# The head of the first mixer: chunks in another order, first K group in halves, sums kept in PSUM, one pass through SBUF

## The chip, the cores and the metric

The kernel is one program on one core of a Trainium2 chip. The metric is the device time of one execution in microseconds (us). A core has five engines with an instruction stream each: TensorE (PE) for matmuls, VectorE (DVE) and ScalarE (ACT) for elementwise work, GpSimdE (POOL), and SyncE (SP), which here only issues DMA transfers. Each engine runs its stream in program order and waits on semaphores that other engines and transfers raise.

## The reference

A trunk of two layers works on one sequence of 256 frames with 2048 features, all in float32. Each layer is a mixer and an MLP, each behind a modulated norm. Cut to what the change touches:

```python
c_act = jax.nn.silu(c)
mod = jnp.einsum('bd,de->be', c_act, mod_w[layer]) + mod_b[layer]
sh1, sc1, g1, sh2, sc2, g2 = jnp.split(mod, 6, axis=-1)
h = rms_norm(x, norm_mix_w[layer]) * (1.0 + sc1) + sh1
...
proj = jnp.einsum('btd,de->bte', h, w_in)
gq, gk, gv, gz, gb, ga, aq, ak, av = split_sizes(proj, AB_SPLITS)
o_a = gated_deltanet(gq, gk, gv, gz, gb, ga, ...)
o_b = chunk_band_attention(aq, ak, av, ...)
x = x + g1 * (concatenate([o_a, o_b]) @ w_out)
```

The head of the first mixer is everything up to the end of `proj`: norm, the first modulation sums, and the product of h with a 2048 x 7184 matrix, in column blocks of 512. The rest (output projection, MLP, the second layer with a state-space mixer) is the same in both kernels.

## The kernel before, in words

**Products.** x lies in SBUF with features on partitions, as four tiles `x[cb]` of 512 features. The contraction over 2048 features is cut in four K groups (`kg` 0 to 3). A weight block of 512 columns comes as four chunks, one for each K group; a chunk is 128 x 2048 float32, 1 MB. There are 14 blocks: the gated-delta ones (GK, GQ, GV, GZ and each +1, told below as k0, q0, v0, k1, q1, v1) as "b" chunks, whose products lie with features on partitions, and the attention ones (AQ, AK, AV and +1: aq, ak, av, aq1 and so on) as "a" chunks, with frames on partitions. A product is done at full precision in one of two ways. *Split*: the weight half (128 x 1024) is cast by ACT to a short type, `wh` (L317), DVE subtracts that from the raw half to get the rest, `wl` (L321), and the same is done to the activations (a unit `u` with high and low part); then PE runs three matmuls for one product, 256 columns wide for b, 512 for a. *Whole*: one float32 matmul on the raw chunk and the unsplit activation `hw`; the trace records each float32 matmul of a b chunk twice. `loader` loads and splits a chunk, `b_item` and `a_item` emit it.

**Modulation.** A column f of modulation vector v is a sum over a 128 x 2048 row of 1 MB with silu(c), broadcast as `crow`: `mod_job` loads the row and DVE does it in one instruction with an accumulator (L439). The head needs shift (v = 0) and scale (v = 1) for 16 columns each, four columns for each K group. In the beginning eight rows are summed, then `norm_unit` makes group 0's unit in the steps L862 (x times scale times R, the inverse norm), L864 (ACT adds the shift) and L865 (the low part).

**Order.** Then for K group 0, 1 and 2 come eight chunks, in the order k0, q0, v0, k1, q1, v1, aq, ak. k0 and q0 keep their sums in PSUM (`held`); for the other six the product of each group is taken out to SBUF, copied by ACT the first time (L1590) and added by DVE the two other times (L1592). Between the chunks the generator `modgen` loads and sums a modulation row for each chunk, eight for the next K group. The last group (from `partial_item(3, 0)`) ends each block in turn: a convolution for b blocks, a norm and transposes for a blocks, and then the delta-rule and attention work as background tasks between chunks. Other blocks (av, aq1, ak1, av1, GZ, GZ+1) run all four chunks there, one after the other.

**Buffers and queues.** Raw chunks and modulation rows share a pool of four buffers of 1 MB (`rawp`); all of them are loaded through SP's queue, in program order, and a load waits at SP's head until the last reader of its buffer is done. Only `pin` and `pin_mod` fix the order of a few instructions; else a scheduler with priorities (`self.priority(20)` for sums) places them on DVE and ACT.

Of the kernel before, what the change touches and what calls it, by code (L numbers as in the profile page):

```python
# [10 lines left out]
F32 = mybir.dt.float32  # L11
# [101 lines left out]
class Trunk:  # L113
# [8 lines left out]
    def __init__(self, tc, ctx, ins, out):  # L122
# [7 lines left out]
        self.u_p = pool("up", 18)  # L130
# [9 lines left out]
        self.ahead = []  # L140
        self.pin_mod = 0
# [174 lines left out]
    def split_steps(self, src, hi, lo, pin=False):  # L316
        a = self.nc.scalar.copy(hi, src)  # L317
        if pin:
            self.tc.keep_in_program_order(a)
        yield  # L320
        b = self.nc.vector.tensor_tensor(lo, src, hi.bitcast(F32), op=ALU.subtract)  # L321
        if pin:
            self.tc.keep_in_program_order(b)
        yield
# [13 lines left out]
    def constants(self):  # L338
# [7 lines left out]
        cact = self.const([P, 16], "cact")  # L346
# [21 lines left out]
    def constants2(self):  # L368
# [3 lines left out]
        for n, f in (("gconv", 0.5), ("gnw", 0.5), ("sconv", 0.5), ("sconv_b", 0.5), ("qnw", P ** -0.5)):  # L372
            nc.vector.tensor_scalar(col(n), col(n), f, None, op0=ALU.mult)
# [50 lines left out]

    def mod_job(self, layer, vs, fs, step):


        nc = self.nc
        key = ("mix", layer) if vs[0] < 3 else ("mlp", layer)
        for f0 in range(fs.start, fs.stop, step):  # L430
            s = slice(f0, f0 + step)
            for f in range(f0, f0 + step):
                for v in vs:
                    t = self.mod[v % 3, key]
                    raw = self.raw_p.tile([P, 2048], F32, tag="raw", name=self.nm("mraw"))
                    nc.sync.dma_start(raw, self.i["mod"][layer, v, f])
                    yield
                    with self.priority(20):
                        x = nc.vector.scalar_tensor_tensor(raw, raw, 1.0, self.crow, op0=ALU.mult, op1=ALU.mult, accum_out=t[:, f : f + 1])  # L439
                    if self.pin_mod > 0:  # L440
                        self.pin_mod -= 1
                        self.tc.keep_in_program_order(x)
                    if f < s.stop - 1 or v != vs[-1]:
                        yield
            for v in vs:
                t = self.mod[v % 3, key][:, s]
                nc.vector.tensor_tensor(t, t, self.modb[:, layer, v, s], op=ALU.add)
                if v % 3 == 1:
                    nc.vector.scalar_tensor_tensor(t, t, 1.0, self.nw[key][:, s], op0=ALU.add, op1=ALU.mult)
                self.ready[v % 3, key] = f0 + step  # L450
# [22 lines left out]
    def loader(self, src, whole=False):  # L473
# [4 lines left out]
        res = []  # L478

        def load():  # L480
            raw = self.raw_p.tile([P, 2048], F32, tag="raw", name=self.nm("raw"))
            nc.sync.dma_start(raw, src)
            for hf in range(2):
                r = raw[:, 1024 * hf : 1024 * hf + 1024]
# [16 lines left out]
    def b_item(self, ps, src, act, first, last, after=None, whole=False):  # L501

        load, ws = self.loader(src, whole)

        def run():
            o_, (u, x) = ps(), act()
            for hf, (wh, wl) in enumerate(self.tiles(ws, 512)):
# [301 lines left out]
    def sumsq(self, cb, b, late=False):  # L809
# [3 lines left out]
        x = self.x[cb][:, 2 * b : 2 * b + 2]  # L813
        if cb == 3:
# [34 lines left out]
    def norm_unit(self, r, cb, key, acts, whole=False):  # L849
# [4 lines left out]
        x = []  # L854
        for b in range(2):
            h = self.s2([P, 2, SEQ], tag="hf")
            if whole:
                x.append(self.s2([P, 2, SEQ], tag="hw"))
            for f in range(2):
# [6 lines left out]
                if whole:  # L866
                    nc.scalar.activation(x[b][:, f], h[:, f], AF.Identity, bias=shift[:, col])
            if b == 0:
                yield
        acts.append((p, x))  # L870
# [63 lines left out]
    def conv(self, ps, tiles, w, bias, part=None):  # L934

        nc = self.nc
        dst = self.unit()
# [294 lines left out]
    def att_qk(self, ps, nw, part=None):  # L1232
# [19 lines left out]
        res = self.unit()  # L1252
# [9 lines left out]
    def att_v(self, ps):  # L1262
        v = self.unit(shape=[P, 2, 4, P])
        for t in range(2):
            self.nc.scalar.copy(v[:, t].rearrange("p h d -> p (h d)"), ps[t])
# [271 lines left out]
    def run(self):  # L1537
# [7 lines left out]
        for layer in range(2):  # L1545
            self.mod_start(layer)
        for t in range(4):
            nc.sync.dma_start(self.x[t].rearrange("p f t -> p (f t)"), i["x"][t])
        for cb in range(4):
            for b in range(2):  # L1550
                self.sumsq(cb, b)
        first = self.mod_job(0, (0, 1), range(0, 4), 2)
# [259 lines left out]
```

## Time and profile before

| | us |
|---|---|
| runs of the kernel before, median (lowest, highest) | 2715.22 (2714.29, 2719.38) |
| the profiled execution | 2719.37 |
| its span, first to last instruction | 2717.6 |
| PE busy in the span | 2665.0 |
| mean granted TensorE clock | 0.998 |

The page of the profile gives the busy time of each engine, the chain of work that ended last, and groups of instructions. A timeline row reads: start, duration, engine, line, operation, out<-in, shapes, count, and in brackets the idle time ahead of it with what ended it. A row of the windows view reads: stretch and its length, then for PE, PEld (PE's weight loads), DVE, ACT and POOL the busy time with the number of instructions in brackets, the granted clock, the DMA share and GB/s. A row of the chain of waits reads: start, duration, what was on the chain.

### The profile page before, as it was taken

To read this page: it belongs to the slowest core of one execution; us is meant where nothing else is said; L and a number is where in the kernel's file an instruction comes from. 1 tells how busy PE (TensorE), PEld (TensorE's weight loads), DVE (VectorE), ACT (ScalarE), POOL (GpSimd) and SP (SyncE) were. 2 spreads that over 40 slices of the span, in tenths; PEclk is the share of its full clock that TensorE was granted. 3 is DMA by queue.
4 is the path that set the end of the run, shared out by engine and by line. 5 is a ranking of instruction groups with operands and counts; after the bars stand their busy time and mean duration, and the time that the engine had idled before them with its cause. 6 is when DMAs were issued, how large, how long until landed. Compare 5 with 4: busy or idle time off the path is not lost.

```text
span 2717.6 us, 39677 instructions
## 1 busy us (share of the span) xinstructions
PE 2665.0 (98%) x15664; PEld 2350.4 (86%) x15664; DVE 2147.6 (79%) x3081; ACT 1351.2 (50%) x1976; POOL 24.5 (1%) x98
## 2 busy tenths in 40 slices
PE   5999999999999999999999999999999999999999
PEld 5887989888888888888888888888888888888888
DVE  7998998987888888889889876897777855555554
ACT  3444454546445354454556544665555354454452
POOL 1000000000000000000000000000000000000000
PEclk9999999999999999999999999999999999999999
DMA  9986487867899898988456665554558855555554
GB/s 341 353 325 235 172 301 272 294 241 282 322 339 328 328 336 330 333 331 307 165 185 217 217 234 200 203 185 172 196 177 293 324 201 188 188 191 193 186 192 134
DMA packets 100459, 680.06 MB, mean 250 GB/s; under 512 B 11185, under 2 KB 14513, under 8 KB 19377
## 3 DMA queue, kind: packets, MB, share of 16 engines
q1 hardware_dynamic: 95376, 669.07, 68.5%
q10 hardware_dynamic: 4896, 8.46, 1.0%
q8 instruction: 123, 2.02, 0.3%
q14 instruction: 64, 0.52, 0.1%
HBM read 675.33 MB, written 2.16 MB: 249 GB/s over the span
## 4 chain that ended last, share of the span: by engine, by line
PE 90%; DVE 6%; DMA 1%; ACT 1%; issue 1%; SPq 0%; ACTq 0%; DVEq 0%
PE pw L308 70%; PE pg L308 13%; PE pm L311 4%; PE pm L308 3%; DVE mraw L439 2%; DVE wl L321 1%; PE pm L314 1%; DMA mraw<-in_mod_dram 1%; DVE u L1592 0%; ACT wh L317 0%; DVE hf L862 0%; ACT pm L1042 0%; DMA raw<-in_w_ab_dram 0%; DMA x<-in_x_dram 0%; DVE u L865 0%
## 5 line engine op out<-in xcount | busy, mean ns | idle before, releaser
L317 ACT CAST wh<-raw 128x1024 fp32r<-128x1024 f32 x870 | 907.1, 1051 | 1031.6 <-PE pw L308 732.9
L321 DVE TENSOR_TENSOR wl<-raw,wh 128x1024 fp32r<-128x1024 f32 x870 | 1048.7, 1220 | 463.8 <-ACT wh L317 349.6
L308 PE MATMUL pw<-u,wh 128*128 128x512 f32 x5584 | 1321.6, 391 | 2.6 <-DVE pad L973 1.9
L308 PEld LDWEIGHTS pw<-u,wh 128*128 128x128 f32 x5584 | 1032.2, 188 | 208.2 <-issue 3.3
L308 PEld LDWEIGHTS pw<-u,wl 128*128 128x128 f32 x5584 | 702.3, 191 | 21.3 <-issue 2.1
L308 PE MATMUL pw<-u,wl 128*128 128x256 f32 x5584 | 714.5, 283 | 0.3 <-DVE wl L321 0.3
L439 DVE SCALAR_TENSOR_TENSOR mraw<-mraw,crow 128x2048 f32<-128x2048 f32 x192 | 438.0, 2283 | 17.8 <-DMA mraw<-in_mod_dram 17.5
L308 PE MATMUL pg<-wh,u 128*128 128x512 f32 x864 | 281.6, 397 | 0.0
L308 PEld LDWEIGHTS pg<-wh,u 128*128 128x128 f32 x864 | 161.9, 188 | 32.1 <-issue 0.5
L925 DVE SCALAR_TENSOR_TENSOR x<-pw,mod,x 128x256 f32<-128x256 f32 x352 | 161.1, 478 | 22.6 <-PE pw L308 20.3
L308 PE MATMUL pg<-wl,u 128*128 128x512 f32 x432 | 169.9, 393 | 0.7 <-DVE wl L321 0.5
L308 PE MATMUL pg<-u,wh 128*128 128x256 f32 x672 | 124.6, 285 | 0.0
L308 PEld LDWEIGHTS pg<-u,wh 128*128 128x128 f32 x672 | 105.7, 192 | 0.3
L308 PEld LDWEIGHTS pg<-wl,u 128*128 128x128 f32 x432 | 81.4, 188 | 17.6 <-DVE wl L321 2.1
L308 PE MATMUL pg<-u,wl 128*128 128x256 f32 x336 | 95.3, 284 | 0.0
L308 PE MATMUL pm<-u,wh 128*128 128x256 f32 (+1 forms) x304 | 64.6, 310 | 19.2 <-ACT wh L317 19.2
L308 PEld LDWEIGHTS pm<-u,wh 128*128 128x128 f32 x304 | 49.1, 198 | 20.3 <-ACT wh L317 20.0
L308 PEld LDWEIGHTS pg<-u,wl 128*128 128x128 f32 x336 | 64.4, 192 | 0.1
L984 DVE SCALAR_TENSOR_TENSOR u<-pad,cst,u 128x256 f32<-128x256 f32 x144 | 60.6, 477 | 3.3 <-ACT u L978 3.2
L864 ACT ACTIVATE u<-hf,mod 128x256 fp32r<-128x256 f32 x64 | 29.3, 502 | 53.0 <-DVE hf L862 53.0
L1504 ACT ACTIVATE rl<-rs 128x512 f32<-128x512 f32 x64 | 40.4, 632 | 18.9 <-DVE rs L1499 14.4
L308 PE MATMUL pm<-u,wl 128*128 128x256 f32 x176 | 46.1, 290 | 3.1 <-DVE wl L321 3.1
(299 smaller groups left out, 1580.5 us busy)
## 6 DMA issues: line engine op xcount, KB each, us to landing
raw<-in_w_dram SPq DMA_DIRECT2D x256, 1024.0 KB, 5.0
mraw<-in_mod_dram SPq DMA_DIRECT2D x192, 1024.0 KB, 6.0
raw<-in_w_ab_dram SPq DMA_DIRECT2D x56, 1024.0 KB, 5.7
raw<-in_w_ssd_dram SPq DMA_DIRECT2D x48, 1024.0 KB, 4.9
raw<-in_w_sz_dram SPq DMA_DIRECT2D x32, 1024.0 KB, 4.9
raw<-in_wo_ssd_dram SPq DMA_DIRECT2D x32, 1024.0 KB, 4.8
raw<-in_wo_ab_dram SPq DMA_DIRECT2D x16, 1024.0 KB, 5.2
sE<-sd_rowd ACTq DMA_DIRECT2D x32, 256.0 KB, 4.9
```

The costliest lines, as they stand in the source:

```text
L308: self.nc.tensor.matmul(o, a, b, start=start, stop=stop, skip_group_check=True)
L311: self.nc.tensor.matmul(o, lhsT, rhs, start=True, stop=True, skip_group_check=True)
L314: self.nc.tensor.transpose(o, a, self.ident[:k, :k])
L317: a = self.nc.scalar.copy(hi, src)
L321: b = self.nc.vector.tensor_tensor(lo, src, hi.bitcast(F32), op=ALU.subtract)
L439: x = nc.vector.scalar_tensor_tensor(raw, raw, 1.0, self.crow, op0=ALU.mult, op1=ALU.mult, accum_out=t[:, f : f + 1])
L864: nc.scalar.activation(hi, h[:, f], AF.Identity, bias=shift[:, col])
L925: nc.vector.scalar_tensor_tensor(x[:, 2 * b + f], ps[:, f, n], g[:, 2 * cb + f : 2 * cb + f + 1], x[:, 2 * b + f], op0=ALU.mult, op1=ALU.add)
L984: nc.vector.scalar_tensor_tensor(h, pad[:, f, 1 + q : 257 + q], w[:, q, j : j + 1], h, op0=ALU.mult, op1=ALU.add)
L1504: nc.scalar.activation(rl, lo, AF.Relu)
```

## The change

The head is written anew. The parts:

- One more buffer in the pool of units (18 to 19). A flag `in_order` fixes the order on SP, DVE and ACT as written, until the first chunk of the last group. A flag `in_units` has weight chunks of K groups 0 and 1 loaded as two halves of 0.5 MB into buffers of the unit pool, not of `rawp`; from group 2 on they go to `rawp` again.
- Before the first product four modulation rows are loaded in place of eight (columns 0 and 1). Scale column 0 comes from an extra input `mod0`, the same weights turned, and is summed by PE in 16 matmuls with one column each (`mod_pe`); `mod_sum` is the DVE sum, `mod_fin` adds bias and factors.
- Group 0's unit is made by `norm_first`: x times R on DVE, scale and shift by ACT into `hw`, then the split. Its first half (256 features) suffices for the first halves of the chunks k0, q0, v0 and k1, which run first. Columns 2 and 3 are summed between them.
- Sequence, eight chunks a group: group 0 the second halves of v0 and k1, then of k0 and q0, then q1, v1, aq, ak; group 1 aq, ak, k0, q0, av (K group 0 and 1) and aq1 (0 and 1); group 2 av, aq1, k0, q0, v0 (1 and 2), k1 (1 and 2). So v0, k1, q1, v1, aq, ak, av and aq1 pass through SBUF once each, by an ACT copy; their last add is part of the block's end.
- The last group goes k0, q0, v0, n_item (the narrow block of gates), k1, aq (2 and 3), ak (2 and 3), av, q1 (1 to 3), v1 (1 to 3), aq1, and then as before.
- Whole chunks: five before, at the last group of k1, q1, v1, aq and ak. Ten after, two of them as two halves: the first halves of k0 and v0, q1 and aq in group 0, aq in group 1, av in group 2, and in the last group k0, k1, aq, q1 and v1.

```diff
-        self.u_p = pool("up", 18)
+        self.u_p = pool("up", 19)
...
+    def mod_pe(self, raw, o):
+        for k in range(16):
+            self.mmx(o, raw[:, k * P : k * P + P], self.cact[:, k : k + 1], k == 0, k == 15)
...
+            if units:
+                raw = [self.unit(shape=[P, 1024]) for _ in hfs]
+                for hf, r in zip(hfs, raw):
+                    self.dma(r, src[:, 1024 * hf : 1024 * hf + 1024])
+            else:
+                raw = self.raw_p.tile([P, 2048], F32, tag="raw", name=self.nm("raw"))
+                self.dma(raw, src)
+                raw = [raw[:, 1024 * hf : 1024 * hf + 1024] for hf in hfs]
...
+    def norm_first(self, cb, key, acts, now=False):
...
+        for b in range(2):
+            self.ordered(nc.vector.tensor_tensor(x[b], self.x[cb][:, 2 * b : 2 * b + 2], self.row(self.R, 2), op=ALU.mult))
+            if now and b == 0:
+                yield
+        yield
+        for b in range(2):
+            for f in range(2):
+                col = slice(cb * 4 + 2 * b + f, cb * 4 + 2 * b + f + 1)
+                self.ordered(nc.scalar.activation(x[b][:, f], x[b][:, f], AF.Identity, scale=scale[:, col], bias=shift[:, col]))
+            self.split(x[b], p[b][:, :, 0], p[b][:, :, 1])
...
+            for n, (name, k, keep) in enumerate(seq):
+                chunk(name, k, n in whole, (1,) if kg == 0 and n < 4 else (0, 1), keep)
+                if n == 0:
+                    self.tail()
+                due = n if kg else (0, 1, 1, 2, 4, 5, 7, 7)[n]
+                load(due + 2)
+                if n == 3:
+                    unit.step()
+                sums(due)
...
+        chunk("k0", 0, True, (0,))
+        raws = [self.mod_load(mod[0, 0, 2])]
+        chunk("q0", 0, False, (0,))
+        raws.append(self.mod_load(mod[0, 1, 2]))
+        self.mod_sum(raws[0], 0, 0, 2)
+        chunk("v0", 0, True, (0,))
+        raws += [self.mod_load(mod[0, v, 3]) for v in range(2)]
+        self.mod_sum(raws[1], 0, 1, 2)
...
+        chunk("k1", 0, False, (0,))
+        for v in range(2):
+            self.mod_sum(raws[2 + v], 0, v, 3)
...
+        group(0, [("v0", 0, False), ("k1", 0, False), ("k0", 0, True), ("q0", 0, True),
+                  ("q1", 0, False), ("v1", 0, False), ("aq", 0, True), ("ak", 0, True)], (4, 6))
+        group(1, [("aq", 1, False), ("ak", 1, False), ("k0", 1, True), ("q0", 1, True),
+                  ("av", 0, True), ("av", 1, True), ("aq1", 0, True), ("aq1", 1, True)], (0,))
+        self.in_units = False
+        group(2, [("av", 2, False), ("aq1", 2, False), ("k0", 2, True), ("q0", 2, True),
+                  ("v0", 1, True), ("v0", 2, True), ("k1", 1, True), ("k1", 2, True)], (0,))
...
+        chunk("k0", 3, True)
+        self.tail()
+        self.in_order = False
+        chunk("q0", 3)
+        chunk("v0", 3)
         self.n_item(i["w_gb"], get, 16, self.gdn_gates)
+        chunk("k1", 3, True)
+        for kg in (2, 3):
+            chunk("aq", kg, kg == 3)
+        for kg in (2, 3):
+            chunk("ak", kg)
```

In `group` the third entry of a chunk says that its sum stays in PSUM, and the last argument lists the whole chunks by place.

SP's loads in the first group of the changed kernel (mraw are modulation rows, u from in_w_ab the half chunks of q0, v0, k1 and then v0's second half):

```order
L454 DMA mraw_274<-in_mod_dram 128x2048
L454 DMA u_276<-in_w_ab_dram 128x1024
L454 DMA mraw_292<-in_mod_dram 128x2048
L454 DMA u_295<-in_w_ab_dram 128x1024
L454 DMA mraw_323<-in_mod_dram 128x2048
L454 DMA mraw_325<-in_mod_dram 128x2048
L454 DMA u_331<-in_w_ab_dram 128x1024
```

Weights and rows now alternate from the first chunk on, where before eight rows stood ahead of the first weight chunk; k1's half (u_331) is behind both rows of column 3.

DVE in the same place, from the split of k1's half on (wl are the low parts of weights, mod_123 and mod_124 the shift and the scale, u_217 the low part of the second half of group 0's unit):

```order
L323 TENSOR_TENSOR wl_334<-u_331,wh_333 128x1024
L435 SCALAR_TENSOR_TENSOR mraw_323,mod_123<-mraw_323,crow 128x2048
L435 SCALAR_TENSOR_TENSOR mraw_325,mod_124<-mraw_325,crow 128x2048
L448 TENSOR_TENSOR mod_123<-mod_123,cst 128x1
L448 TENSOR_TENSOR mod_124<-mod_124,cst 128x1
L450 SCALAR_TENSOR_TENSOR mod_124<-mod_124,cst 128x1
L323 TENSOR_TENSOR u_217<-hw_219,u_217 128x2x256
```

Both sums of column 3 now stand between the split of k1's first half and the unit's second half.

SP's loads in group 2, first before, then of the changed kernel (raw are weight chunks of 1 MB):

```order
L482 DMA raw_1276<-in_w_ab_dram 128x2048
L436 DMA mraw_1312<-in_mod_dram 128x2048
L482 DMA raw_1339<-in_w_ab_dram 128x2048
L436 DMA mraw_1373<-in_mod_dram 128x2048
L482 DMA raw_1400<-in_w_ab_dram 128x2048
```

```order
L454 DMA raw_1041<-in_w_ab_dram 128x2048
L454 DMA mraw_1075<-in_mod_dram 128x2048
L454 DMA mraw_1077<-in_mod_dram 128x2048
L454 DMA raw_1079<-in_w_ab_dram 128x2048
L454 DMA mraw_1097<-in_mod_dram 128x2048
L454 DMA raw_1100<-in_w_ab_dram 128x2048
L454 DMA mraw_1137<-in_mod_dram 128x2048
L454 DMA raw_1143<-in_w_ab_dram 128x2048
```

Both alternate, but the changed kernel starts group 2 with two rows between its first two weights, av's chunk (raw_1041, whole) and aq1's (raw_1079). The buffers of `rawp` fall to them accordingly: before, a weight load follows the weight two loads back in its buffer (raw_1400 after raw_1276), now the weight directly before it (raw_1100 after raw_1079, raw_1143 after raw_1100), and mraw_1097 follows raw_1041.

More of the change, by code (lines that the diff above doesn't have):

```diff
@@ L847, in norm_bc, with norm_unit @@
         return ps
[L849 removed]
+    def norm_first(self, cb, key, acts, now=False):
+        nc = self.nc
+        scale, shift = self.mod[1, key], self.mod[0, key]
+        p, x = self.pair(), [self.s2([P, 2, SEQ], tag="hw") for _ in range(2)]
+        if now:
+            acts.append((p, x))
+        for b in range(2):
[8 more added lines that the diff above has]
+            self.split(x[b], p[b][:, :, 0], p[b][:, :, 1])
+            if b == 0:
+                yield
+        if not now:
+            acts.append((p, x))
+    def norm_unit(self, r, cb, key, acts):
         nc = self.nc
```

255 lines of the change are left out of this document (154 added, 101 removed).

## The prediction

> **What bounds the kernel now.** I read the page's totals and chain first, then windows of the head, then the timeline and the chain of waits there.
>
> ```profile
> PE 2665.0 (98%) x15664; PEld 2350.4 (86%) x15664; DVE 2147.6 (79%) x3081; ACT 1351.2 (50%) x1976; POOL 24.5 (1%) x98
> ...
> PE 90%; DVE 6%; DMA 1%; ACT 1%; issue 1%; SPq 0%; ACTq 0%; DVEq 0%
> 30.00:40.00 10.00, 0.00 (x0) 0.00 (x0) 9.37 (x16) 1.33 (x2) 0.00 (x0) 1.00 0.96 346
> 40.16:88.10 47.94, 47.90 (x336) 45.74 (x336) 39.54 (x45) 21.39 (x30) 0.00 (x0) 1.00 0.94 343
> 88.10:137.50 49.40, 46.65 (x339) 43.68 (x338) 47.02 (x59) 20.57 (x24) 0.00 (x0) 1.00 0.93 348
> 137.50:187.43 49.93, 47.18 (x341) 44.01 (x340) 48.91 (x61) 20.29 (x26) 0.00 (x0) 1.00 0.93 344
> 187.43:245.20 57.77, 57.36 (x308) 44.84 (x309) 54.14 (x102) 28.26 (x61) 0.62 (x6) 1.00 0.68 251
> 40.16 1.22 PE L308 MATMUL pm<-u,wh 128*128 128x256 f32 x4 [17.47 <-ACT wh L317]
> ```
>
> TensorE (PE) carries 90% of the chain and is busy 98% of the span, so time can come only from the few places where it isn't. The window 30 to 40 us shows the largest: no matmul, while VectorE (DVE) works 9.37 of 10 us on modulation sums. The weight matmuls start at 40.16 us, after 17.47 us of idleness. The three windows behind it are K groups 0 to 2, eight chunks of 1 MB each; in the second and third DVE is busy 47 and 49 us of 49 and 50, so there DVE limits along with PE:
>
> ```profile
> 176.85 2.22 DVE mraw L439 x2
> 179.17 2.36 DVE wl L321 x2
> 181.53 1.20 DVE u L1592 x2
> ...
> 187.43 11.30 PE pm L308 x92
> ```
>
> These rows of the chain of waits put a modulation sum (2.2 us), two splits (2.36) and two adds of partial sums (1.20) in a row for each chunk. From 187.43 on the chain is PE's.
>
> **Unit prices.**
>
> ```profile
> 40.00:45.00 5.00, 4.80 (x20) 4.51 (x21) 4.86 (x7) 3.59 (x7) 0.00 (x0) 1.00 0.83 287
> 45.00:50.00 5.00, 5.00 (x41) 5.00 (x41) 3.93 (x5) 2.10 (x2) 0.00 (x0) 1.00 1.01 382
> 91.67 0.40 PE L308 MATMUL pm<-u,wh 128*128 128x256 f32 x2
> ...
> 92.02 0.40 PE L308 MATMUL pm<-u,wh 128*128 128x256 f32 x2
> 87.63 0.39 PE L308 MATMUL pg<-wh,u 128*128 128x512 f32 x1
> 87.86 0.39 PE L308 MATMUL pg<-wl,u 128*128 128x512 f32 x1
> ...
> 229.75 7.03 PE L308 MATMUL pg<-raw,hw 128*128 128x512 f32 x16
> L308 PE MATMUL pg<-hw,raw 128*128 128x256 f32 x96 | 21.9, 379 | 0.0
> ```
>
> Between 91.67 and 92.02 three 256-column matmuls start, so 0.12 us each; 87.63 to 87.86 gives 0.227 us for 512 columns. A split "b" chunk is 48 of the first, 5.76 us; a split "a" chunk 24 of the second, 5.45 us. A whole "a" chunk took 7.03 us with its tail, some 6.86 by its starts; a whole "b" chunk is 32 records at 21.9/96 = 0.228 us busy, 0.216 by starts, so 6.9 us. Whole costs PE +1.15 (b) and +1.41 (a) and spares DVE two splits. After 17 us of idleness the first 5 us hold 20 matmuls, the next 5 hold 41: a cold start loses 2.5 us.
>
> **The change, part by part.**
>
> *1. Start.*
>
> ```profile
> L436 SPq DMA_DIRECT2D mraw<-in_mod_dram x1: 536/536/536, 4.9 to 4.9; - x1
> ...
> DMA to landing us min/median/max: 14.3/14.3/14.3
> 18.80 2.29 DVE L439 SCALAR_TENSOR_TENSOR mraw<-mraw,crow 128x2048 f32<-128x2048 f32 x1
> 11.85 3.55 PE L308 MATMUL pm<-ones,sq 128*128 128x1 f32 x16
> 22.73 0.37 ACT L1570 COPY R<-pm 128x256 f32<-128x256 f32 x1 [11.01 <-PE pm L314]
> 27.53 0.91 ACT L864 ACTIVATE u<-hf,mod 128x256 fp32r<-128x256 f32 x2 [4.43 <-DVE hf L862]
> L1592 DVE TENSOR_TENSOR u<-pg,u 128x512 f32<-128x512 f32 x22 | 14.3, 682 | 0.9 <-PE pg L308 0.9
> ```
>
> Now eight modulation rows must be summed before the first product; after it four, one of them by PE. The queue holds the same bytes, so the fourth row lands as now: issued at 4.9, 14.3 us later, 19.2. Its DVE sum of 2.29 ends at 21.5. PE's sum is 16 matmuls, 32 records; at 3.55/16 us each 7.1 us from the landing of its row at about 13.3, done at 20.4 and hidden. R, now copied at 22.73 because its steps stand among sums, comes at about 21.5. Then a product of x and R (priced by the 682 ns row), four small adds and factors (0.16 each) with their hand-overs, and a ScalarE (ACT) scale and shift (0.91/2): 24.2 us against 40.16, **-16.0**. Ends: 23 if R is early, 27 if R stays at 23.1 and each hand-over costs more.
>
> *2. First group.* PE gets four half chunks, two of them whole: 12.7 us and the 2.5 of a cold start reach to 39.4. What is late next is the second half-unit (hw_219, u_217): it needs modulation columns 2 and 3, on DVE the sums mraw_323 and mraw_325 of column 3 stand behind the split of k1's half (wl_334), and that half (u_331) is loaded behind both rows on SP.
>
> ```profile
> GB/s 0 0 0 119 240 310 365 433 380 372 402 432 402 462 447 447 402 432 432 432 432 417 365 391 485 444 417 447 432 417 417 417 462 179 104 74 119 432 462 402
> ```
>
> A full queue moves some 430 GB/s (first row, 40 slices of the first 22 us), 2.43 us for 1.05 MB. Between the row at 19.2 and the end of k1's half stand four rows and four halves, six such: landing 33.8. Cast and split take 2.3, two sums of 2.28 reach 40.7, the unit's scaling and split 42.6, the first weights' cast and split for it 45.2: a wait of about **6 us**. Ends: 0 if hw_219 is in time, 9 if landings slip by one row.
>
> After 17.47 us of idleness PE is cold, after 1.71 it isn't:
>
> ```profile
> 90.18 0.74 PE L308 MATMUL pm<-u,wh 128*128 128x256 f32 x4 [1.71 <-ACT wh L317]
> ```
>
> The granted clock reads 1.00 in both places, and no row here shows 6 us. It lies nearer to 1.71, so I count no second cold start; the other end is 2.5 us. The Trainium skill, "TensorE: Matmul & The Clock Gate", section "What's actually happening", speaks against this: it has the clock halved after an idle window of some 3.4 us. By that rule the sum would be 2.5 us higher. The loss of 2.5 us in the window from 40 agrees with the rule's size.
>
> *3. Whole chunks.* 24 chunks before the last group now cost 18x5.76 + 6x5.45 = 136.4. After: 14 b and 10 a, 135.1, plus whole: 2 b and 3 a, 2.3 + 4.2; 141.6 together, **+5.2**. From there on one more whole b, one less whole a, four chunks turned from a into b: **+0.9**.
>
> *4. One pass through SBUF.* 22 adds of 682 ns, 14.3 us, and about as much in splits leave DVE before the last group. That gain is worth at most what PE loses now: 187.43 - 40.16 = 147.3 us for 136.4 of work, 10.9 lost, 2.5 of it cold.
>
> *5. Group 2's loads.* Here a new wait is made.
>
> ```profile
> 153.32 2.00 ACT L317 CAST wh<-raw 128x1024 fp32r<-128x1024 f32 x2 [5.84 <-DMA raw<-in_w_ab_dram]
> 154.40 2.36 DVE L321 TENSOR_TENSOR wl<-raw,wh 128x1024 fp32r<-128x1024 f32 x2 [0.81 <-ACT wh L317]
> DMA to landing us min/median/max: 4.8/4.8/4.8
> DMA to landing us min/median/max: 5.6/6.7/7.0
> ```
>
> In the program of before, a weight load waits for the second split of the weight two loads back (raw_1400 for that of raw_1276): two loads are under way in turn. In group 2 of after each waits for that of the load directly before (raw_1143 for raw_1100, raw_1213 for raw_1143 and so on); the modulation rows turn in the other three buffers. So a chunk's period is issue 0.1 + landing + splits. A load alone lands in 4.8 us (window 234:242); from landing, cast and both splits end at 154.40 + 2.36 = 156.76, 3.44 after 153.32. Sum 8.4 us against 5.76 of PE. Before it, mraw_1097 waits for PE's end of av's whole chunk, and raw_1100 is queued behind it on SP. Group 2's work is 6.86 + 5.45 + 6x5.76 = 46.9, so groups 0 and 1 end at 24.2 + (141.6 - 46.9) + 2.5 + 6 = 127.4. The whole av chunk ends at 134.3, raw_1100 lands 4.8 + 2.4 later behind its row, its splits end near 145.1; five periods on raw_1407's end at 187.1, and the whole k0 chunk of the last group lands at **192.0** and starts. Group 2 has 46.9 us of work in 64.6: **17.7** lost. Ends: 0 if the loop doesn't hold, and 10.3 us a period if loads land in 6.7 as in 140:160, where modulation rows run beside them: 12 us more. A pause of 2.6 us in each, even if each chunk then lost the 2.5 us of a cold start, stays within 8.4 (5.76 + 2.5 = 8.3). I take 8.4, since the rows are issued right behind the weight before, long landed when the next weight is issued.
>
> The Trainium skill, "DMA: Bandwidth & Descriptors", section "Anatomy of one DMA", gives about 2.0 us and bytes at 436 GB/s for a transfer (on another issue path): 4.4 us for 1 MB, where the trace has 4.8. By an estimate from it the period is 8.0 and the sum 2.5 us lower; the measured row stands.
>
> *6. Last group to the end of the head.*
>
> ```profile
> PE pm L314 <- DVE aq L1250: 2.8, 2, 2.0
> PE pw L308 <- DVE pad L973: 1.9, 1, 1.9
> ```
>
> Convolutions, norms and transposes of k0, q0, v0, aq and ak now meet within fewer chunks. Walking the queues I find PE behind DVE or ACT five times: n_item behind v0's pads, aq behind a copy, gates and ak's split, av's, aq's transposes. The nearest rows, waits of these kinds (PE's waits over the whole span: in total, times, longest), give about 2 us each, the transposes more: 12 us against some 5 lost in the same stretch now. Some 3 come back later, where the convolutions are then done: **+4**; ends -5 (all hidden) and +10 (none given back, one more). DVE is busy 54.14 of 57.77 us there, so there is little cover.
>
> **Sum.** Start of the last group: 187.4 to about 192, which is -16.0 start, +5.2 work, +15.3 waits (2.5 + 6 + 17.7 against 10.9) = +4.5; +0.9; +4: **+9.4 us**. The profiled execution took 2719.37 us (span 2717.6, 1.8 around it), the median is 4.2 lower; so 2728.8 by the profile, 2724.6 by the median, told as **2725**.
>
> **Rivals.**
>
> *The loop of loads doesn't decide (faster).* One mechanism: loads of group 2 start two deep. It decides at a period of 5.76 us, above which each of some seven periods costs the difference. With two under way it is 4.2 and PE is the bound: the last group starts near 176, -11.4, then +0.9 and +4: -6.5, **2709**. For it: DVE has slack in group 2. Against: the waits in the program.
>
> *Loads at 6.7 us (slower still).* Periods of 10.3: +12, **2737**. For: the 140:160 row; against: there a second load is always in flight.
>
> *No waits behind the last group.* Then -5 in place of +4: **2716**, no change.
>
> *The change doesn't bring its start.* If R or the sums stay where they are, near 33, 9 us come back on top: **2734**.
>
> **How the numbers follow.** My forecast, a loop that binds and waits behind it, 0.52; loop doesn't decide 0.18; no waits behind 0.14; loads at 6.7 and a late start 0.08 each. A difference under 0.2% (5.4 us) is about what a measurement here can't tell from none: 2709.8 to 2720.6. Faster: most of the first rival, whose other terms spread a few us around 2709, 0.14, and 0.06 from the low ends of the third and of the forecast: 0.2. Same: the rest of these and most of the third, 0.23. Slower 0.57. The range goes from the first rival with its start 2 us better and part of the wait of part 2 spared, 2705, to 2738, which takes in the loads at 6.7 and the late start.
>
> **What would show it.** The first weight matmul at 24 us (part 1); idleness before 45 ended by u or wh (2); in group 2 SP issues weight loads 8.4 us apart, ACT waits for raw about 5 us in each and PE 2 to 3 (5): with periods under 6 the first rival is right. The last group starting at 192 (sum), and the same blocks' convolutions and transposes in the waits to 260 (6). Wrong would be the sum if DVE, not the load, ended group 2's waits, or if waits of the stretch behind the head change by more than 10 us.

## The result, and the profile after

| | before | after |
|---|---|---|
| median of the runs, us | 2715.56 (2714.29 to 2719.38, 4 runs) | 2744.63 (2741.67 to 2746.56, 4 runs) |
| ratio, 95% interval | | 1.0106 (1.0093 to 1.0118) |
| profiled execution, span | 2719.37, 2717.6 | 2743.88, 2742.1 |

The changed kernel is 1.06% slower, 29.1 us by the medians. 2725 was forecast, slower too, but the range ended at 2738. The two profiled executions differ by 24.5 us; the other 4.6 us lie in where they stand among their runs (before 3.8 above its median, after 0.75 below). All sums of stretches below are of the profiled executions.

The page of the profile after: totals by engine, and the chain of work that ended last.

```profile
PE 2687.2 (98%) x15620; PEld 2360.4 (86%) x15620; DVE 2122.5 (77%) x3053; ACT 1346.7 (49%) x1968; POOL 24.9 (1%) x98
...
PE 88%; DVE 6%; DMA 3%; ACT 2%; issue 1%; SPq 0%; ACTq 0%; DVEq 0%
```

DVE works 25 us less, as meant, and the time rose: on the chain the share of DMA went from 1% to 3% and that of ACT from 1% to 2%. The windows view of after says where, cut at the first weight matmul, behind K group 0, behind group 1, at the last group and at the end of the head:

```profile
0.00:23.19 23.19, 12.84 (x58) 12.09 (x58) 15.31 (x35) 8.83 (x17) 8.37 (x38) 1.00 0.92 369
23.19:85.30 62.11, 56.46 (x296) 48.17 (x296) 45.51 (x66) 20.83 (x31) 0.00 (x0) 0.92 0.94 375
85.30:130.92 45.62, 45.62 (x233) 37.08 (x232) 38.28 (x46) 19.91 (x24) 0.00 (x0) 1.00 0.92 361
130.92:195.55 64.63, 54.93 (x329) 47.84 (x328) 37.15 (x43) 18.12 (x22) 0.00 (x0) 0.89 0.64 236
195.55:516.30 320.75, 304.87 (x2065) 273.53 (x2064) 277.33 (x580) 156.09 (x394) 14.29 (x38) 0.99 0.65 237
516.30:2742.10 2225.80, 2212.51 (x12646) 1941.72 (x12644) 1708.89 (x2286) 1122.87 (x1481) 2.29 (x22) 1.00 0.68 243
```

And of before, the last two stretches:

```profile
187.43:491.26 303.83, 299.59 (x1962) 265.06 (x1963) 272.74 (x570) 154.69 (x393) 13.91 (x38) 0.99 0.69 245
491.26:2717.60 2226.34, 2214.97 (x12655) 1944.01 (x12653) 1710.33 (x2291) 1123.44 (x1484) 2.27 (x22) 1.00 0.68 243
```

| stretch | before, us | after, us | change | forecast |
|---|---|---|---|---|
| to the first weight matmul | 40.16 | 23.19 | -17.0 | -16.0 |
| groups 0 and 1 | 97.06 | 107.73 | +10.7 | +6.1 |
| group 2 | 50.21 | 64.63 | +14.4 | +14.4 |
| last group to the end of the head | 303.83 | 320.75 | +16.9 | +4.9 |
| the rest | 2226.34 | 2225.80 | -0.5 | 0 |
| sum | | | +24.5 | +9.4 |

(Groups 0 and 1 of before end at 137.22, its group 2 is counted to 187.43 as in the prediction. That is 1.9 us into the last group: its first chunk starts behind 185.56. Counted from there, group 2 of before takes 48.34 us and its last stretch 305.70, so the last two changes are +16.29 and +15.05.) The change works at the start and is lost three times over. Behind the head nothing differs. Of the 15.1 us by which the forecast was too low, 12.0 lie in the last group and 4.6 in groups 0 and 1.

Below, PE's *loss* in a stretch is the sum, over its matmuls, of the time from one start to the next beyond what is usual for that kind (the value under which the shortest fifth of its kind lies in the two profiles). It counts idle time and slow matmuls alike. From the last group's start to the end of the head it rose from 20.8 us (from 185.56) to 35.0; PE's work by the same prices rose by 1.5.

**Group 2.** SP's rows of after, weight loads of group 2 from the fourth on, the ACT rows that wait for two of them, and the splits on DVE before two of the loads:

```profile
149.02 0.33 SPq L454 DMA_DIRECT2D raw<-in_w_ab_dram  x1
...
157.49 0.33 SPq L454 DMA_DIRECT2D raw<-in_w_ab_dram  x1
...
165.89 0.33 SPq L454 DMA_DIRECT2D raw<-in_w_ab_dram  x1
...
174.23 0.33 SPq L454 DMA_DIRECT2D raw<-in_w_ab_dram  x1
```

```profile
154.02 2.00 ACT L319 CAST wh<-raw 128x1024 fp32r<-128x1024 f32 x2 [5.51 <-DMA raw<-in_w_ab_dram]
...
162.42 1.99 ACT L319 CAST wh<-raw 128x1024 fp32r<-128x1024 f32 x2 [5.43 <-DMA raw<-in_w_ab_dram]
```

```profile
146.63 2.36 DVE L323 TENSOR_TENSOR wl<-raw,wh 128x1024 fp32r<-128x1024 f32 x2 [7.81 <-ACT wh L319]
...
155.10 2.36 DVE L323 TENSOR_TENSOR wl<-raw,wh 128x1024 fp32r<-128x1024 f32 x2 [3.52 <-ACT wh L319]
```

The loads start 8.47, 8.40 and 8.34 us apart, each just when the splits before it end (148.99 and 157.46 here); the DMA share falls to 0.64 in the group, and ACT waits 5.5 us for bytes. PE loses 18.2 us there; 9.7 of it is idle time, the rest slow matmuls behind the pauses.

**First group.** PE's timeline of after, and windows (PEclk, the granted clock, stands third from the end):

```profile
23.19 5.85 PE L309 MATMUL pm<-hw,u 128*128 128x256 f32 x16 [2.17 <-ACT hw L902]
...
36.53 0.50 PE L309 MATMUL pg<-u,wh 128*128 128x256 f32 x2 [1.16 <-ACT wh L319]
37.79 0.58 PE L309 MATMUL pg<-u,wl 128*128 128x256 f32 x1 [0.76 <-DVE wl L323]
...
45.07 0.80 PE L309 MATMUL pg<-u,wh 128*128 128x256 f32 x2 [2.90 <-ACT wh L319]
46.42 0.58 PE L309 MATMUL pg<-u,wl 128*128 128x256 f32 x1 [0.55 <-DVE wl L323]
```

```profile
28.70:35.00 6.30, 6.30 (x42) 5.87 (x40) 3.03 (x7) 0.00 (x0) 0.00 (x0) 1.00 1.01 417
35.00:41.30 6.30, 4.38 (x20) 3.81 (x19) 4.79 (x4) 1.55 (x2) 0.00 (x0) 0.73 1.03 415
41.30:51.30 10.00, 6.55 (x33) 6.05 (x32) 8.19 (x18) 4.41 (x7) 0.00 (x0) 0.67 0.94 364
51.30:85.30 34.00, 33.73 (x193) 27.92 (x192) 25.58 (x35) 12.77 (x19) 0.00 (x0) 1.00 0.89 354
```

The idle time is 5.4 us (forecast 6), but in two pieces, and behind each the clock fell: 0.73 and 0.67, with matmuls 0.213 us apart until 41.2 and 51.3. The chain of waits tells the two pieces apart:

```profile
22.36 13.04 DMA u<-in_w_ab_dram
35.43 1.05 ACT wh L319
36.51 1.23 DVE wl L323
37.73 4.42 DVE mraw L435 x4
42.58 0.61 ACT hw L902
...
45.15 1.23 DVE wl L323
```

The first is a wait for k1's half itself: its bytes are there at 35.4, where the forecast had 33.8. Only the second is the forecast one, for the two sums of column 3 and the second half-unit behind them.

**Last group.** The first 64 us of the last group in after, and DVE's groups there, after and before (xcount, then busy us):

```profile
195.67:260.00 64.33, 57.23 (x308) 46.47 (x307) 62.22 (x132) 33.12 (x70) 1.14 (x9) 1.00 0.72 277
```

```profile
L1014 DVE SCALAR_TENSOR_TENSOR u<-pad,cst,u 128x256 f32<-128x256 f32 x48 | 20.7, 475 | 0.1
L323 DVE TENSOR_TENSOR wl<-raw,wh 128x1024 fp32r<-128x1024 f32 x14 | 16.8, 1216 | 1.6 <-ACT wh L319 1.6
L435 DVE SCALAR_TENSOR_TENSOR mraw<-mraw,crow 128x2048 f32<-128x2048 f32 x6 | 13.7, 2280 | 0.0
```

```profile
L321 DVE TENSOR_TENSOR wl<-raw,wh 128x1024 fp32r<-128x1024 f32 x13 | 15.4, 1218 | 0.2 <-ACT wh L317 0.2
L959 DVE SCALAR_TENSOR_TENSOR u<-pad,cst,u 128x256 f32<-128x256 f32 x36 | 14.8, 476 | 0.1
L439 DVE SCALAR_TENSOR_TENSOR mraw<-mraw,crow 128x2048 f32<-128x2048 f32 x6 | 13.7, 2286 | 1.0 <-DMA mraw<-in_mod_dram 1.0
```

A fourth convolution (k1's) has come into the stretch, twelve products more; DVE is busy 62.2 of 64.3 us. It was not idle there before either: 54.14 of 57.77 us in the row of the prediction, where PE still worked 57.36. PE's waits in after from 195.67 to 400, the longest of them:

```profile
PE pg L309 <- DVE wl L323: 3.0, 1, 3.0
PE pm L312 <- ACT gu L1101: 2.3, 1, 2.3
PE pg L309 <- ACT nb L683: 2.2, 1, 2.2
PE pm L315 <- DVE aq L1305: 1.8, 1, 1.8
```

### The profile page after: what moved, and what is told of

Its sections match the earlier page's. It is cut to its first block, busy times and chain, and to the rows that moved or that the text cites. A ratio compares the mean times of both kernels' runs of the same rounds, so it can differ in the third digit from the quotient of the medians.

```text
span 2742.1 us, 39564 instructions
## 1 busy us (share of the span) xinstructions
PE 2687.2 (98%) x15620; PEld 2360.4 (86%) x15620; DVE 2122.5 (77%) x3053; ACT 1346.7 (49%) x1968; POOL 24.9 (1%) x98
## 4 chain that ended last, share of the span: by engine, by line
PE 88%; DVE 6%; DMA 3%; ACT 2%; issue 1%; SPq 0%; ACTq 0%; DVEq 0%
PE pw L309 69%; PE pg L309 13%; PE pm L312 3%; DVE wl L323 2%; PE pm L309 2%; DVE mraw L435 1%; DMA mraw<-in_mod_dram 1%; DMA raw<-in_w_ab_dram 1%; PE pm L315 1%; ACT wh L319 1%; DMA u<-in_w_ab_dram 1%; DVE u L1014 0%; ACT pm L1097 0%; DMA sE<-sd_rowd 0%; DVE u L1039 0%
## 5 line engine op out<-in xcount | busy, mean ns | idle before, releaser
L323 DVE TENSOR_TENSOR wl<-raw,wh 128x1024 fp32r<-128x1024 f32 x836 | 1008.8, 1220 | 489.1 <-ACT wh L319 377.5
L319 ACT CAST wh<-raw 128x1024 fp32r<-128x1024 f32 x836 | 872.7, 1051 | 1021.4 <-PE pw L309 730.1
L309 PE MATMUL pg<-wh,u 128*128 128x512 f32 x832 | 272.3, 399 | 5.9 <-DVE wl L323 3.0
L309 PEld LDWEIGHTS pg<-wh,u 128*128 128x128 f32 x832 | 156.4, 189 | 40.0 <-ACT pg L1299 3.5
L309 PE MATMUL pg<-wl,u 128*128 128x512 f32 x416 | 163.6, 393 | 1.3 <-DVE wl L323 1.3
L309 PEld LDWEIGHTS pg<-u,wl 128*128 128x128 f32 x312 | 63.5, 204 | 5.2 <-DVE wl L323 5.2
L309 PE MATMUL pm<-u,wh 128*128 128x256 f32 (+1 forms) x256 | 55.3, 312 | 3.6 <-ACT wh L319 3.6
L1558 DVE TENSOR_TENSOR rs<-pw,rs 128x512 f32<-128x512 f32 x64 | 43.7, 683 | 4.7 <-ACT rs L1557 4.7
L1557 ACT COPY rs<-pw 128x512 f32<-128x512 f32 x64 | 36.9, 577 | 17.3 <-PE pw L309 17.3
L309 PEld LDWEIGHTS pm<-u,wh 128*128 128x128 f32 x256 | 40.7, 195 | 4.5 <-ACT wh L319 4.2
```

Of the source, the lines that this page charges most:

```text
L309: self.nc.tensor.matmul(o, a, b, start=start, stop=stop, skip_group_check=True)
L1557: nc.scalar.copy(lo, ps[:, :, 1])
L1558: nc.vector.tensor_tensor(lo, ps[:, :, 0], lo, op=ALU.add)
```

## The experiments

Each is the changed kernel with one edit, or with several where the text says so; `...` stands for lines left out. Medians go with the ratio to the kernel before and its interval; the medians of before beside them were 2714.6 to 2715.7.

**e1_swap: the buffers of group 2.**

```diff
+                due = n if kg else (0, 1, 1, 2, 4, 5, 7, 7)[n]
+                if kg == 2:
+                    sums(due)
                 chunk(name, k, n in whole, (1,) if kg == 0 and n < 4 else (0, 1), keep)
...
-                due = n if kg else (0, 1, 1, 2, 4, 5, 7, 7)[n]
...
-                sums(due)
+                if kg < 2:
+                    sums(due)
```

> Group 2 alone: the sum of a modulation row stands before the chunk, not behind it, so weight loads and rows change places in the four buffers and a weight load no longer waits for the split of the weight directly before it; nothing is left out. Theory (one buffer for all weights of group 2 costs the wait there): SP issues weights of group 2 some 6 us apart in place of 8.4, PE loses about 4 us in group 2 in place of 18, the last group starts near 182 in place of 195.7, total near 2731 if the rest stays. Rival (DVE or ACT would limit group 2 anyway, or the load's 4.9 us is exposed in another way): PE still loses over 12 us there, total over 2740.

2734.01 us, 1.0063 (1.0048 to 1.0078). Group 2 in the windows view:

```profile
130.62:182.90 52.28, 49.50 (x330) 43.73 (x328) 37.12 (x46) 20.62 (x26) 0.00 (x0) 0.97 0.85 314
```

Group 2 takes 52.3 us in place of 64.6, PE's loss there falls from 18.2 to 5.8, the clock goes back to 0.97. A buffer order that two lines of code decide was worth 12.4 us; 10.6 of them reach the end by the medians, since the last group to the head's end now takes 324.0.

**e2_k1first: the order of loads in the first group.**

```diff
-        raws += [self.mod_load(mod[0, v, 3]) for v in range(2)]
         self.mod_sum(raws[1], 0, 1, 2)
...
         chunk("k1", 0, False, (0,))
+        raws += [self.mod_load(mod[0, v, 3]) for v in range(2)]
```

> First group alone: the two modulation rows of column 3 are loaded behind k1's first half, not before it; nothing is left out. Theory (the pauses at 35 to 46 us come from SP's order, and each makes PE cold for some 4 us more): k1's half lands near 30 in place of 35.4, PE runs on to about 38, one pause of some 3 us and one cold stretch in place of two; PE loses some 8 us from its start to the end of group 0 in place of 14, total 5 to 7 us lower, near 2739. Rival (the later wait for the halves behind takes it all): the matmuls of the second half-unit still begin near 46, total within 1 us of 2744.6.

2738.66 us, 1.0087 (1.0070 to 1.0104): 6.0 us less, as expected. One pause is left, 2.1 and 0.8 us at 41 and 42.6; loss from the start to the end of group 0 falls from 14.1 to 10.3 (8 was expected), and the last group starts 3.6 us earlier.

**e3_nomodpe: the TensorE sum undone.**

```diff
-        raws = [self.mod_load(mod[0, 0, 0]), self.mod_load(i["mod0"]), self.mod_load(mod[0, 0, 1])]
+        raws = [self.mod_load(mod[0, 0, 0]), self.mod_load(mod[0, 1, 0]), self.mod_load(mod[0, 0, 1])]
...
-        self.mod_pe(raws[1], sums)
         self.mod_sum(raws[0], 0, 0, 0)
+        self.mod_sum(raws[1], 0, 1, 0)
```

> The modulation sum on TensorE alone is undone: scale column 0 is summed by DVE from the ordinary row, 2.3 us more on DVE ahead of the first product; nothing is left out. Theory (the first product waits for DVE, but the pause at 42 to 46 is set by loads): first matmul 2 us later at about 25.4, second half-unit's matmuls still near 46, total within 1.5 us of 2744.6. Rival (the start counts to the end): total 2 to 3 us higher.

2746.84 us, 1.0118 (1.0102 to 1.0133). The first product is at 24.59, 1.4 us later, but group 1 ends at 130.23, not later than with the TensorE sum (130.92): by then nothing of it is left. The total is 2.2 us higher, as the rival had it, but the two intervals overlap; in the profile the difference lies in group 2 (66.5 for 64.6 us) and the last stretch (321.9 for 320.75). Whether the early start counts to the end stays undecided.

**e4b_spread and e10_k1later: other places for block ends.** e4b moves av's last chunk ahead of v0's and k1's last behind ak's in the changed kernel; e10 (on e6_both, which is e1 and e2 together) moves only k1's. The edit of e10:

```diff
-        chunk("k1", 3, True)
         for kg in (2, 3):
             chunk("aq", kg, kg == 3)
         for kg in (2, 3):
             chunk("ak", kg)
+        chunk("k1", 3, True)
```

> Last group alone: av's last chunk moves ahead of v0's, k1's last chunk behind ak's, so that block ends with convolutions stand further apart; nothing is left out. Theory (after the last group's start DVE is full, 62.2 us busy of 64.3, with the convolutions of k0, q0, v0 and k1 and the norms of aq and ak, and PE waits for its splits): PE's loss from the last group's start to the end of the head falls from 35 to about 28, total near 2738. Rival (the sum of DVE's work is the same and the waits only move): loss 33 to 37, total within 2 us.

> e6_both, and k1's last chunk alone moves behind ak's; av stays where it is; nothing is left out. Theory (the twelve products of k1's convolution, some 8 us of DVE work, stand in the full stretch and make PE wait): PE's loss in the first sixteen chunks behind the last group's start falls from 18 to about 10, total 4 to 8 us below e6_both. Rival (it stands elsewhere in the way, since the wait is for what ends last in a row of dependent steps): loss within 3 us of 18, total within 3 us of e6_both.

2746.35 us, 1.0117 (1.0102 to 1.0132), and 2732.24 us, 1.0063 (1.0049 to 1.0076). Neither brought what the theory expected: e4b's total is that of the changed kernel within 2 us, as its rival had it, though PE's loss rose from 35.0 to 39.0; e10 is 4 us worse than e6_both, which its rival did not expect either, and its loss in the first sixteen chunks rose from 18 to 25. The longest PE wait behind the last group's start, in e4b and in e10:

```profile
PE pg L309 <- DVE pad L1000: 12.4, 1, 12.4
```

```profile
PE pg L309 <- ACT cvt L1016: 9.8, 1, 9.8
```

Several waits became one. In e4b PE's next block waits for a convolution's add, which reads the sums out of PSUM (L1000) and stands in DVE's queue behind a modulation sum and the products of a convolution. In e10 the profile names an ACT step (L1016); the same add ends at 208.07 there and PE starts at 208.21, so I take it for the same wait, but it isn't shown. Moving a block end moved the wait.

**e6_both, e5_whole, e8_norows: DVE's load in the last group.** e6 is e1 and e2 together. On it, e5 makes two chunks whole, and e8 keeps modulation rows away, their loads too:

```diff
-        chunk("q0", 3)
-        chunk("v0", 3)
+        chunk("q0", 3, True)
+        chunk("v0", 3, True)
```

```diff
-        self.rate, self.rate2 = 0.25, 1.1
+        self.rate, self.rate2 = 0.0, 1.1
...
         chunk("av", 3)
+        self.rate = 0.5
```

> The edits of e1_swap and e2_k1first together; nothing is left out. Theory (two separate waits of the head, which add up): 10.6 and 6.0 us less than 2744.6, near 2728, first group's loss near 8 and group 2's near 6. Rival (what the head gains early is taken back behind the last group's start, since DVE is the limit there): the stretch behind it is 5 us or more longer than the 321 us of the changed kernel, total over 2732.

> e6_both, and the last chunks of q0 and v0 are done whole: PE works 2.3 us more, DVE makes four splits (4.9 us) less behind the last group's start; nothing is left out. Theory (DVE is the limit from there to the first attention norms): PE's loss falls by 5 to 7 us there, total 3 to 5 us below e6_both. Rival (the waits are PE's own or for buffers): total 1 to 3 us above e6_both.

> e6_both, and no modulation rows are loaded or summed from the last group's start to the chunk of av (six of 2.28 us on DVE stand there now); they follow later at a higher rate; nothing is left out. Theory (DVE's fullness behind the last group's start makes PE wait): PE's loss in the first sixteen chunks behind it falls from 18 to about 8, some of it comes back later, total 4 to 8 us below e6_both. Rival (PE waits there for PSUM banks or for chains of small steps, whatever DVE's load): loss within 3 us, total within 2 us of e6_both.

2728.09 us, 1.0043 (1.0029 to 1.0058); 2726.02, 1.0036 (1.0023 to 1.0049); 2720.20, 1.0020 (1.0011 to 1.0029). The two waits add up in e6. The last group to the end of the head takes 322.6, 315.4 and 314.7 us: 7 to 8 us less with less for DVE to do at the beginning. In e8 this reaches the total, 7.9 us. In e5 only 2.1 us do, which the intervals don't tell from none: its last group starts 1.6 us later, and the part behind the head takes 3.0 us more. The loss in the first sixteen chunks fell only from 18.2 to 15.2 and 14.9 (for e8 about 8 was expected), the rest further behind.

**e13_pads and e14_notaps: buffers or amount.** On e6_both, three convolution buffers for two (`bufs=3`), or no products with the earlier taps at all, `for q in range(0)`.

> e6_both, and three buffers instead of two for the padded input of a convolution (in the mixer of the second layer too); nothing is left out. Theory (block ends queue for these buffers: a convolution can take its sums out of PSUM only when an earlier one has let go of a buffer, and PE waits for the PSUM bank): the stretch behind the last group's start is 5 to 10 us shorter than e6_both's 322.6. Rival (DVE's amount of work there, not the buffers): within 2 us of 322.6.

> e6_both, and the three products with the earlier taps are left out of the six convolutions of the first mixer (72 DVE instructions of 0.48 us, 34 us in all, 48 of them in the full stretch behind the last group's start); loads, splits and matmuls stay. Theory (DVE's work and its place in the queue make PE wait there): PE's loss behind the last group's start falls from 36.8 us to 22 or less, the stretch from 322.6 to 308 or less. Rival (the waits come from PSUM banks and chains of ACT and PE steps): loss over 30, stretch over 316.

2725.57 us, 1.0040 (1.0025 to 1.0055), stretch 320.5 for 322.6: the buffers are worth 2 us at most. e14: 2714.46, 0.9996 (0.9986 to 1.0006), stretch 307.2, PE's loss in it 22.0 for 36.8. The first 66 us of the last group, e6_both and e14:

```profile
179.00:245.00 66.00, 60.99 (x317) 49.46 (x316) 63.50 (x131) 32.44 (x70) 1.14 (x9) 0.95 0.71 265
```

```profile
179.00:245.00 66.00, 64.06 (x345) 51.94 (x344) 48.35 (x91) 40.23 (x113) 1.13 (x9) 1.00 0.77 283
```

DVE falls from 63.5 to 48.4 us busy, PE rises by 3. DVE's work makes the waits, not the buffers. Whether its amount does or its place in the queue isn't separated: e14 leaves less for DVE to do and makes each convolution shorter too, and the kernel before lost little beside a DVE that was busy 54.14 of 57.77 us. Of the 14.8 us of loss that go, 5.7 lie in the first sixteen chunks and 9.1 behind, where e14 also leaves out the products of q1 and v1.

**e7_start, e9_best: the new start with the old sequence.** e7 has e6_both's start and halves, but the chunks in the order of before; e9 also takes up the old way of loading and a free order on DVE from group 1 on.

```diff
+        group(1, [(n, 1, held(n)) for n in ("k0", "q0", "v0", "k1", "q1", "v1", "aq", "ak")], ())
...
+        chunk("q0", 3)
+        self.a_block(w, AV, get, lambda ps: put("v0", self.att_v(ps)))
+        chunk("v0", 3)
```

> The new start and halves of the first group with the edits of e6_both, but the chunks of K groups 0 to 3 in the order of the kernel before, with their partial sums added in SBUF each time and only its five whole chunks and the two halves at the start; nothing is left out. Theory (the later loss comes from the new sequence: whole chunks, one-buffer loads and the convolutions that meet in the last group): start at 23.5, first group's loss near 8, the stretch behind the last group's start near the 306 us of the kernel before, total near 2706. Rival (any early start is lost later, because loads or DVE limit the groups): total over 2712.

> e7_start, but from K group 1 on weights go to the four 1 MB buffers again, rows are pumped between the matmuls and DVE's order is free, as in the kernel before; only the start and group 0 stay new. Nothing is left out. Theory (the pinned order and the loads cost e7's K groups 1 and 2 their 21 us of loss; the new start is worth having once the rest is as before): start 23.3, first group's loss 10, groups 1 and 2 lose 4 us each, last group starts near 181 and the stretch to the end of the head takes 303 to 306 us; total 5 to 8 us below the kernel before, near 2708. Rival (an early start finds loads or DVE behind in any order): groups 1 and 2 lose 10 us and more each, total at or over the kernel before.

2724.52 us, 1.0031 (1.0020 to 1.0042), and 2712.59, 0.9990 (0.9981 to 0.9999). e7's last stretch takes 302.4 us, 305.70 in the kernel before, so the 320.75 of the changed kernel belong to the new sequence. Its groups 1 and 2 lose 9.3 and 11.5 us: in DVE's pinned order the splits that PE wants stand behind modulation sums and adds (from 113.2 to 119.4 us two sums, two adds and the low part of a unit stand ahead of two splits, and PE loses 4.8 us at once). e9 undoes this order and the loads in halves together, so the share of each isn't shown. e9, group 0 to 2 in the windows view:

```profile
23.41:85.94 62.53, 53.69 (x319) 49.39 (x320) 54.01 (x74) 27.86 (x38) 0.00 (x0) 0.89 0.93 363
85.94:131.40 45.46, 45.46 (x337) 43.57 (x336) 41.39 (x48) 19.37 (x22) 0.00 (x0) 1.00 0.93 348
131.40:179.31 47.91, 45.73 (x338) 43.54 (x336) 43.45 (x50) 17.71 (x21) 0.00 (x0) 1.00 0.90 335
```

0.2 and 2.6 us lost in groups 1 and 2. e9 is the one version that leaves nothing out and whose interval lies below the kernel before, by 2.6 us where 5 to 8 were expected; of the 16.7 us that it starts earlier, group 0 takes 14.6 (62.5 for 47.9): PE loses 16.7 us in it, where 10 was expected.

**e11_warm: a warm PE at the start.** On e9:

```diff
+        spare = self.pm([P, 512])[:, :SEQ]
+        for _ in range(4):
+            self.mmx(spare, self.x[0][:, 0, :P], self.x[0][:, 1], True, True)
```

> e9_best, and PE does four more float32 matmuls of 256 columns (eight records) into a PSUM buffer that nobody reads, in its pause of 2.6 us ahead of the first weight matmul; nothing of the computation is left out. Theory (the slow matmuls at the start are a cold state that ends after some 4 to 5 us of matmuls, whatever they are): the weight matmuls at 23 us reach 0.12 us each about 2.5 us earlier, the first group's loss is 1 to 2 us lower. Rival (the slow rate comes from the weight work itself, its first loads or operands): the first weight matmuls take as long as before, loss unchanged; the first weight matmul is at most 0.5 us later in both.

2714.50 us, 0.9996 (0.9987 to 1.0005). The first sixteen weight records, e9 and e11:

```profile
23.41 5.59 PE L309 MATMUL pm<-hw,u 128*128 128x256 f32 x16 [2.23 <-ACT hw L902]
28.65 0.82 PE L309 MATMUL pm<-u,wh 128*128 128x256 f32 x4
```

```profile
20.95 3.62 PE L309 MATMUL pm<-x 128*128 128x256 f32 x8
24.36 4.58 PE L309 MATMUL pm<-hw,u 128*128 128x256 f32 x16
28.59 0.83 PE L309 MATMUL pm<-u,wh 128*128 128x256 f32 x4
```

They take 4.2 us in place of 5.2: matmuls on other operands warm PE too, here for 1.0 us of the 2.5 that were expected. The first was 0.95 us later, so q0's half begins at the same time, and the total gains nothing.

**e12_nowhole: the whole chunks of groups 0 to 2.** On e6_both, the lists `(4, 6)`, `(0,)` and `(0,)` become empty.

> e6_both, and the four chunks of K groups 0 to 2 that were whole (q1 and aq in group 0, aq in group 1, av in group 2) are done split, so that only the halves of k0 and v0 stay whole there: 1.15 + 3 x 1.41 = 5.4 us less work for PE, eight more splits (9.8 us) for DVE; nothing is left out. Theory (whole chunks are an added cost that nothing there needs, as PE loses little in groups 0 and 1): the last group starts 4 to 6 us earlier than in e6_both (179.1), total 3 to 6 us below e6_both. Rival (the whole chunks spare DVE and the loads just enough): PE's loss in groups 0 to 2 rises by 5 us or more, total at or above e6_both.

2725.62 us, 1.0042 (1.0026 to 1.0059). The last group starts at 178.28, 0.8 earlier: of the 5.4 us of work spared, 4.2 come back as loss in group 0's second half (6.5 for 2.3). In PE's stretch this is largely the rival; the total is 2.5 us below e6_both, between the two, and the intervals overlap.

## Why the prediction was right and wrong

- *What bounds, and the sign*: right. PE was the chain (88% of it after), its gaps the only stock, and the change made more of them than it took away. The size was not: +9.4 us forecast, +24.5 in the profiled executions.
- *Part 1, start*: right, 23.19 for 24.2, but e3 shows that the TensorE sum's share is gone by the end of group 1.
- *Part 2, first group*: the idle time was right in its sum (5.4 for 6), partly by luck, since 1.9 us of it was a wait for k1's half, which the forecast had in time. The step "I count no second cold start" was wrong. There were two: the loss from the start to the end of group 0 was 14.1 us for 8.5 (2.5 + 6). I chose by the length of the idle time; the trace has cold matmuls behind 1.16 and 0.76 us with two matmuls between. The Trainium skill's rule, "TensorE: Matmul & The Clock Gate", section "What's actually happening", weighed there, came nearer: a window that runs free and asks how busy PE was, not how long one gap is. With the 2.5 us that the prediction names for it the loss would have been 11.0, for 14.1 measured.
- *Part 3, whole chunks*: counted as 5.2 us of time (the two halves at the start make one chunk of the ten). As work this fits e12, which has 5.4 less, but there the last group starts only 0.8 us earlier: without the whole chunks PE waits for splits instead, so most of the 5.2 wasn't a price in time.
- *Part 4, one pass through SBUF*: DVE works 25 us less, and group 1 runs with PE busy throughout (45.62 us, 49.14 before). But e9 keeps the adds and takes 45.46 us there, so the pass through SBUF wasn't needed for it.
- *Part 5, the loop of loads*: right in place, mechanism and size: 8.4 us a period, 64.63 us for 64.6, a loss of 18.2 for 17.7. e1 shows it by undoing it. That the cold starts stay within the period also held (clock 0.89 there, same 8.4).
- *Part 6, last group to the end of the head*: this step failed, and it holds 12.0 of the 15.1 us that were missing. "12 us of waits against some 5 lost in the same stretch now. Some 3 come back later" made +4. Counted from each kernel's last group on, the first sixteen chunks lost 17.7 us for 8.4 before, and nothing came back: the last sixteen lost 17.3 for 12.4, +4.9 in place of -3. The list of waits was near (five of 12 us forecast, four single ones up to 270 us found, 9.3 together), but the kernel before lost only 1.5 us in its first eight chunks there, where "some 5" had no row behind it. The error was to price each wait singly and to trust that convolutions done early would leave room. What the runs show in its place: the loss belongs to the new sequence (e7: 302.4 us for 320.75) and to DVE's work in it (e14: 15 us of the stretch go with it; e5 and e8: 7 to 8). That a full DVE passes a delay on to later chunks fits e5 and e8, where half or more of the loss that goes lies behind the first sixteen, but isn't shown step by step, and how it divides among single block ends stays open: e4b and e10 only moved it.
- *Median and profile*: I took 4.2 us off for the high profiled execution of before. The one of after was not as high among its runs, so the medians differ by 29.1 us, the profiled executions by 24.5.

## What to carry to other kernels

When an engine's adds are saved by running pieces in another order, look at what the new order does to the pool that feeds them: which buffer the next load falls into decides how many loads are under way, and a loop of one is load plus all that reads it. A stage with an engine at 94% of its time (DVE, 54.14 of 57.77 us) has little room for block ends moved into it, and the loss can show up at other engines and later places. And a pause of PE can cost twice, by its length and by the cold matmuls behind it.

## What the runs showed of the hardware

Cold matmuls come behind pauses much shorter than the 17 us in front of the first: behind 1.16 and 0.76 us within 2.8 us, but not behind 1.71 and 0.52 us at 90 us in the kernel before, with four matmuls between. Where the line runs is not shown. The granted clock doesn't always show the first cold matmuls: it reads 1.00 in after (23.19 to 28.70) and 0.50 in e6_both, where they are as slow:

```profile
23.59:28.90 5.31, 5.31 (x13) 4.24 (x14) 3.62 (x4) 2.10 (x3) 0.00 (x0) 0.50 1.02 408
```
